# Three edits to a hybrid diffusion step in split fp32: another pool for modulated tiles, an operand built beside the output projection, gate and residual one chunk sooner

## The chip, the cores and the metric

The kernel runs on one core of one Trainium2 chip. The metric is the device time of one launch in microseconds (us), the median of several runs; lower is better. The engines of the core work side by side: PE (TensorE) does the matmuls, PEld is its weight load, DVE is VectorE, ACT is ScalarE, POOL is GpSimd, SP is SyncE. Each engine runs its own instructions in order and waits on semaphores for the others. In this kernel SP issues the loads from HBM and POOL issues most of the stores and a few loads.

## The reference

One layer of a network with three kinds of token mixing, for 128 context tokens and 2048 latent tokens of width D = 1024, all in fp32. What matters here is its second half:

```
mix = concat(A, B, C) @ w_out                       # 1024 x 1024
x   = x + gate1 * mix                               # called x1 in the kernel
h   = rmsnorm(x) * (1 + scale2) + shift2            # the modulated tile
x   = x + gate2 * (square(relu(h @ w_ff1)) @ w_ff2) # 1024 x 4096, 4096 x 1024
y   = rmsnorm(x, final_g)
```

shift2, scale2, gate1 and gate2 are vectors of 1024, one set for the context tokens and one for the latent ones. A, B and C are gated linear attention, a depthwise convolution and a gated MLP over chunks; they come ahead of the stages that the change touches.

## The kernel before

**Tiles and arithmetic.** The 2176 tokens are 17 tiles of 128: t = 0 is the context, t = 1 to 16 are latent. Every fp32 matmul operand is held as a pair: hi, a copy on ACT that is rounded to the matmul's type, and lo, the source minus hi, subtracted on DVE or POOL. One product is three matmuls (`mm3`: hi x hi, hi x lo, lo x hi), so lo of the left operand is first wanted by the third matmul. Function `split` (L169 on) does the copy (L171) and the subtract (L172); `split_in_place` (L1168 on) does it with lo over the source (L1169, L1170).

**Stages.** In the profiled execution the projection of the inputs and the mixing take the time up to about 731 us, the output projection lasts to about 1031, FF1 (h @ w_ff1, with a Strassen-like form of seven products p = 0 to 6 on sums of operand blocks) to about 1743, FF2 to 2492, and a tail follows.

**Output projection** (`out_proj`, L754 on, called for t = 16 down to 0). For each tile it loads the mixed tile `mt` (L766), copies it to `mh` on ACT (L767), subtracts `ml` on POOL (L768), loads `x1` (L770), and takes a buffer `tmp` (L772). Then 16 units of 3 matmuls run, 8 for each half of the columns. After each half `done` multiplies by the gate row into `tmp` (L777) and adds into `x1` (L778), on DVE; after the second half it stores x1 (L780), squares and sums (L64), takes the reciprocal root (L160, L161) and scales x1 into `tmp` (L784). The modulated tile is made in `tmp` beside the NEXT tile's matmuls: at unit 12 and after unit 16 `h2_half` transposes four 128 x 128 blocks on PE (L129) and applies scale and shift with four ACT instructions (L64). Tiles go in pairs, even t then odd t. After the odd tile's second half `h2_pair` (L815 on) forms four combinations of both tiles on DVE (L827 to L830) into two tiles `cb`, and POOL issues stores of all to `tb_d` (L822, L831 to L834); these are FF1's right operands, for i = 0 to 6.

**What sets the order.** The program is written as loops, and a list scheduler orders each engine's instructions when the program is built. The buffers of one tag in a pool are handed out strictly in the order in which the program first writes them: an instruction that first writes a buffer is placed after the one that first writes the buffer handed out before it. The load of `mt` is the first write of its buffer. The hand-out orders the placing alone: a load on SP may run as soon as its own buffer is free. `weave` (L149) runs the units in turn and the side items at their unit numbers.

**Pools.** Tag w (23 buffers of 128 x 1024, `wtile`) holds w_out (16), the gate rows, `x1` and `tmp`. Tag T (18, `tunit`) holds `mt`, `mh`, `ml` and `cb`, later FF1's right operands of i < 4, and in FF2 the accumulators `ya`. When the output projection is done pool wp is closed (L1152) and pool fp lies over its memory: tag u (12, `uunit`) for right operands of i >= 4 and for FF2's left operands F, tag v (11, `wunit`) for weights. The first buffers of fp are handed out only behind the last release of wp. `raw` (3 buffers) stages loads, `cacc` (2) and `xp` (3) are work tiles.

**FF1's start** (L1286 on). Left operands are loaded and split (`left_operand`, L1180), the 14 halves of right operands (7 i, two kk each) are loaded by POOL (L1176) and split in place.

**FF2** (`ff2_units`, L1385, loop L1419). 8 chunks c of 512 rows of w_ff2; in each, 5 blocks b of token tiles: four of 4 tiles and one of 1 tile (t = 0). A tile is 24 matmuls in 8 units, 12 for each half of the columns. The four weight pairs of the next chunk are loaded and split during blocks 0 to 3 (`load_ff2`, L1337, split L171 and L172). The left operands F of a block are two pairs, loaded (`load_f`, L1354) and split in place; three such sets fit in tag u. Each half is evicted by ACT in chunk 0 (L1403) and added into `ya` by DVE after that (L1405). In the last chunk `finish` (L1360) multiplies the half by gate2 (L1372), adds x1 (L1373), squares (L1376), and after the second half takes the root and scales twice (L67), then stores. It loads x1 again from `x1_d` into a `raw` buffer.

The functions that the diff touches:

Of the kernel before, what the change touches and what calls it, by code (L numbers as in the profile page):

```python
# [8 lines left out]
F32 = mybir.dt.float32  # L9
# [9 lines left out]
D = 1024  # L19
# [24 lines left out]
def tile_hybrid(  # L44
# [60 lines left out]
    def xp_tile():  # L105
        return rawp.tile([P, 1536], F32, tag="xp", name="xp", bufs=3)
# [4 lines left out]
    def wtile(dt=F32R):  # L111
        return wp.tile([P, D], dt, tag="w", name="w", bufs=23)
# [36 lines left out]
    def weave(units, items):  # L149

        items = sorted(items, key=lambda it: it[0])
        for i, u in enumerate(units):
            while items and items[0][0] <= i:
                items.pop(0)[1]()
            u()
        for _, f in items:
            f()
# [596 lines left out]
    def out_proj(t):  # L754

        cd = 0 if t == 0 else 1
        if cd not in g1rows:
            g1rows[cd] = wtile(F32)
            gate_row(g1rows[cd], 0, cd)
        cq.finish(t)  # L760
        if t == NT - 1:
            hu, mt = hunit()
            mh, ml = hu[:, 0], hu[:, 1]
        else:
            mt, mh, ml = tunit(F32), tunit(), tunit()
        ld.dma_start(out=mt, in_=mix_d[t].rearrange("p k t -> p (k t)"))  # L766
        S.copy(out=mh, in_=mt)  # L767
        G.tensor_tensor(out=ml, in0=mt, in1=mh.bitcast(F32), op=ALU.subtract)  # L768
        x1 = wtile(F32)
        ld.dma_start(out=x1, in_=x_rows(t))  # L770

        tmp = xp_tile()[:, 0:D] if t == 0 else wtile(F32)  # L772

        def done(half):
            def f(pz):
                fs = slice(half * 512, (half + 1) * 512)
                V.tensor_tensor(out=tmp[:, fs], in0=pz, in1=g1rows[cd][:, fs], op=ALU.mult)  # L777
                V.tensor_tensor(out=x1[:, fs], in0=tmp[:, fs], in1=x1[:, fs], op=ALU.add)  # L778
                if half == 1:
                    st.dma_start(out=x1_d[t], in_=x1)  # L780
                    ssq = const.tile([P, 1], F32, name="ssq3", bufs=2)
                    act(tmp, x1, AF.Square, accum_out=ssq)
                    rstd_of(ssq, ssq, D)
                    S.mul(tmp, x1, ssq)  # L784
            return f

        def lhs(k):
            ks = slice(k * P, (k + 1) * P)
            return mh[:, ks], ml[:, ks]

        units = []
        for half in range(2):
            units += mm_units(512, lhs, of_pairs(wo[half]), done(half))

        hs = []

        def h2_half(kq):
            pt = gbank()
            for kk in range(4):
                k = kq * 4 + kk  # L800
                tr(pt[:, kk * P:(kk + 1) * P], tmp[:, k * P:(k + 1) * P])
            hf = tmp.rearrange("p (k t) -> p k t", k=KD)
            for kk in range(4):
                k = kq * 4 + kk
                act(hf[:, k, :], pt[:, kk * P:(kk + 1) * P], AF.Identity, scale=s2[:, k, cd:cd + 1],
                    bias=modc[:, KD + k, cd:cd + 1])
            ks = slice(kq * 4, kq * 4 + 4)
            if t == 0:
                split(hc[0][:, ks], hc[1][:, ks], hf[:, ks])
            elif kq == 1:  # L810
                h2_pair(t, hf)

        return units, [(12, lambda: h2_half(0)), (16, lambda: h2_half(1))]
# [22 lines left out]
    def ticks(n, rate):  # L836
        return [(p_ + 0.5, lambda: cq.tick(rate / n)) for p_ in range(n)]
# [3 lines left out]
    with ExitStack() as p2:  # L841
# [110 lines left out]
        class ConvQueue:  # L952
# [27 lines left out]
            def finish(self, t):  # L980

                while any(t in g[0] for g in self.groups):
                    self.tick(1.0)
                self.credit = 0.0
                while any(t in d[1] for d in self.due):
                    self.tick(0.0)
# [155 lines left out]
    hbs.close()  # L1142
    tp.append(tps.enter_context(tc.tile_pool(name="tp", bufs=1, side="right", reuse_waits="tile")))
    hc = []

    for t in range(NT - 2, -1, -1):
        units, nxt_late = out_proj(t)
        if t == 0:
            hc += [tunit().rearrange("p (k t) -> p k t", k=KD) for _ in range(2)]
        weave(units, late3 + ticks(16, RATE3))  # L1150
        late3 = nxt_late
    wps.close()  # L1152

# [6 lines left out]
    def wunit(dt=F32R):  # L1160
        return fp.tile([P, D], dt, tag="v", name="v", bufs=11)
# [2 lines left out]

    def split_in_place(hi, lo):  # L1168
        S.copy(out=hi, in_=lo.bitcast(F32))  # L1169
        V.tensor_tensor(out=lo, in0=lo.bitcast(F32), in1=hi.bitcast(F32), op=ALU.subtract)  # L1170

    def right_operand(g, i, kk, dst):

        unit = tunit if i < 4 else uunit
        hi, lo = unit(), unit()
        st.dma_start(out=lo.bitcast(F32).rearrange("p (k n) -> p k n", k=2), in_=tb_d[g][:, i, 2 * kk:2 * kk + 2])  # L1176
        split_in_place(hi, lo)
        dst[i, kk] = (hi, lo)

    def left_operand(i):  # L1180

# [101 lines left out]

        return [lambda k=k: unit(k) for k in range(KD)], turn

    TB = [{}, {}]  # L1286
    ORDER = [(i, kk) for i in range(7) for kk in range(2)]
    w, steps = left_operand(0)
    steps[0]()
    steps[1]()  # L1290
    for i, kk in ORDER[:2]:
        right_operand(0, i, kk, TB[0])
    steps[2]()
    for i, kk in ORDER[2:4]:
        right_operand(0, i, kk, TB[0])
# [41 lines left out]
    def load_ff2(f):  # L1337
        rw = raw()
        ld.dma_start(out=rw, in_=w_ff2[0, f * P:(f + 1) * P, :])
        hi, lo = wunit(), wunit()  # L1340
        split(hi, lo, rw)
        return hi, lo

    def load_f(c, b):
# [12 lines left out]

        return out, [lambda p=p: step(p) for p in range(CF // 2)]

    def finish(t, y):  # L1360

        ssq = const.tile([P, 2], F32, name="ssq4", bufs=4)
        x1 = raw()
        ld.dma_start(out=x1, in_=x1_d[t])
        g2c = g2r
        if t == 0:
            g2c = raw()
            gate_row(g2c, 1, 0)

        def half(h):  # L1370
            fs = slice(h * 512, (h + 1) * 512)
            V.tensor_tensor(out=y[:, fs], in0=y[:, fs], in1=g2c[:, fs], op=ALU.mult)  # L1372
            V.tensor_tensor(out=y[:, fs], in0=x1[:, fs], in1=y[:, fs], op=ALU.add)  # L1373
            act(x1[:, fs], y[:, fs], AF.Square, accum_out=ssq[:, h:h + 1])
            if h == 1:
                V.tensor_tensor(out=ssq[:, 0:1], in0=ssq[:, 0:1], in1=ssq[:, 1:2], op=ALU.add)  # L1376
                rstd_of(ssq[:, 0:1], ssq[:, 0:1], D)
                for i in range(2):
                    fs = slice(i * 512, (i + 1) * 512)
                    stt(y[:, fs], y[:, fs], ssq[:, 0:1], fgr[:, fs], ALU.mult, ALU.mult)  # L1380
                    ld.dma_start(out=y_rows(t)[:, fs], in_=y[:, fs])

        return half

    def ff2_units(c, b, F, w2):  # L1385
        units = []
        for j, t in enumerate(blocks[b]):
            js = slice(j * P, (j + 1) * P)
            fin = []

            def unit(h, f, t=t, js=js, fin=fin, box=[]):
                hs = slice(h * 512, (h + 1) * 512)
                if f == 0:
                    box.append((zbank if h == 0 else gbank)())
                py = box[-1]
                fh, fl = F[f // 2]
                mm3(py, fh[:, f % 2, js], fl[:, f % 2, js], w2[f][0][:, hs], w2[f][1][:, hs], f == 0, f == CF - 1)
                if f < CF - 1:
                    return
                if c == 0:  # L1400
                    if h == 0:
                        ya[t] = tunit(F32)
                    S.copy(out=ya[t][:, hs], in_=py)  # L1403
                else:
                    V.tensor_tensor(out=ya[t][:, hs], in0=py, in1=ya[t][:, hs], op=ALU.add)  # L1405
                if c == NC_ - 1:
                    if h == 0:
                        fin.append(finish(t, ya[t]))
                    fin[0](h)

            units += [lambda h=h, f=f, unit=unit: unit(h, f) for h in range(2) for f in range(CF)]
        return units
# [5 lines left out]
    steps[1]()  # L1418
    for c in range(NC_):  # L1419
        w2n = []  # L1420
        for b in range(5):
            units = ff2_units(c, b, F, w2)
            items = []
            nb, ncx = (b + 1, c) if b < 4 else (0, c + 1)
            if ncx < NC_:
                F, steps = load_f(ncx, nb)
                items += zip((3.5, 9.5) if b < 4 else (0, 1), steps)
            if c + 1 < NC_ and b < 4:
                items.append((14.5, lambda f=(c + 1) * CF + b: w2n.append(load_ff2(f))))
            weave(units, items)  # L1430
        w2 = w2n
# [30 lines left out]
```

## Time and profile before

| | us |
|---|---|
| median of 3 runs | 2510.64 |
| lowest and highest run | 2509.28, 2511.52 |
| the profiled execution, its own time | 2516.82 |
| its span, first to last instruction | 2515.1 |

| engine | busy us | share of the span |
|---|---|---|
| PE | 2349.2 | 93% |
| DVE | 1472.8 | 59% |
| ACT | 890.1 | 35% |
| POOL | 436.8 | 17% |

Mean granted PE clock 0.966. The times of rows are microseconds from the start of the span. In a timeline a row is start, length, engine, line, operation, output and inputs by the program's names, shapes, how many instructions run together; in brackets how long the engine sat idle before it and what ended that. Rows of one engine stand for its order; rows of different engines overlap.

### The profile page before, as it was taken

The page shows a single profiled execution, that of the slowest core. Times are in us where ns is not written, and L with a number is a line of the kernel's source. Part 1 is how long each engine was busy: PE and PEld are TensorE (multiplying, and loading weights), DVE is VectorE, ACT ScalarE, POOL GpSimd, SP SyncE. Part 2 cuts the span into 40 slices and gives each one's busy share as a digit, 9 for nine tenths or more (in the row PEclk, how much of TensorE's full clock was granted, in tenths as well). Part 3 has the DMA queues.
Part 4 walks back from the last instruction along what each step waited for, and adds up shares of the span by engine and source line. Part 5 has one row for each costly group of instructions (what it writes and reads, how often), then busy time and mean ns, then how long its engine had stood idle before and what let it go on. Part 6 is the DMA issues. An engine that isn't in the chain of part 4 may idle for free.

```text
span 2515.1 us, 32249 instructions
## 1 busy us (share of the span) xinstructions
PE 2349.2 (93%) x12402; PEld 1921.3 (76%) x12402; DVE 1472.8 (59%) x2492; ACT 890.1 (35%) x1710; POOL 436.8 (17%) x593
## 2 busy tenths in 40 slices
PE   6999999999988777699999899999999999999996
PEld 5788887777766555488888788887878888888885
DVE  5987755878885663555555766655134344344387
ACT  4666764333444344432333433333321011011032
POOL 2332325444423333200000100000000000000001
PEclk9999999999998888799999999999999999999998
DMA  8655635333443444522233533335122122122154
GB/s 277 236 194 195 219 107 165 121 125 130 144 153 130 151 148 167 202 97 91 103 103 105 198 101 106 123 106 176 38 84 88 38 88 84 38 88 84 38 196 152
DMA packets 145321, 326.24 MB, mean 130 GB/s; under 512 B 13349, under 2 KB 58703, under 8 KB 141584
## 3 DMA queue, kind: packets, MB, share of 16 engines
q1 hardware_dynamic: 110640, 191.73, 23.5%
q0 software_dynamic: 34528, 132.46, 14.6%
q8 instruction: 97, 1.59, 0.3%
q14 instruction: 56, 0.46, 0.1%
HBM read 213.24 MB, written 110.90 MB: 129 GB/s over the span
## 4 chain that ended last, share of the span: by engine, by line
PE 62%; DVE 12%; issue 5%; POOL 4%; DMA 2%; ACT 2%; POOLq 0%; SPq 0%; DVEq 0%; ACTq 0%
PE z L126 42%; PE g L126 19%; DVE cacc L67 5%; DMA u<-tb_d 1%; PE g L129 1%; DVE T L67 1%; POOL T L768 1%; DMA u<-f_d 1%; POOL ssq L161 1%; DVE uv L67 1%; DVE T L1373 1%; POOL mv L161 1%; POOL s L161 1%; DVE T L1405 1%; DVE T L1372 0%
## 5 line engine op out<-in xcount | busy, mean ns | idle before, releaser
L126 PE MATMUL z<-w,hb 128*128 128x512 f32 (+1 forms) x2438 | 551.1, 372 | 5.7 <-ACT w L171 3.2
L126 PEld LDWEIGHTS z<-w,hb 128*128 128x128 f32 x2438 | 412.6, 192 | 81.8 <-issue 5.0
L126 PE MATMUL z<-v,u 128*128 128x512 f32 x1632 | 395.0, 391 | 3.5 <-DVE v L172 1.5
L126 PE MATMUL g<-v,u 128*128 128x512 f32 x1632 | 393.6, 391 | 0.0
L126 PEld LDWEIGHTS z<-v,u 128*128 128x128 f32 x1632 | 306.7, 188 | 69.4 <-DVE v L172 2.3
L126 PEld LDWEIGHTS g<-v,u 128*128 128x128 f32 x1632 | 307.7, 189 | 64.0
L126 PE MATMUL z<-T,v 128*128 128x512 f32 x1152 | 286.6, 401 | 29.2 <-ACT T L1169 22.7
L126 PEld LDWEIGHTS z<-T,v 128*128 128x128 f32 x1152 | 217.3, 190 | 84.4 <-ACT T L1169 25.3
L126 PE MATMUL z<-w,T 128*128 128x512 f32 x768 | 212.1, 431 | 65.9 <-ACT T L767 51.2
L126 PE MATMUL z<-u,v 128*128 128x512 f32 x1152 | 269.2, 392 | 0.0
L1169 ACT CAST u<-u 128x1024 fp32r<-128x1024 f32 (+1 forms) x92 | 86.3, 939 | 489.2 <-DMA u<-f_d 330.1
L126 PEld LDWEIGHTS z<-u,v 128*128 128x128 f32 x1152 | 217.6, 189 | 46.5
L126 PEld LDWEIGHTS z<-w,T 128*128 128x128 f32 x768 | 153.4, 207 | 106.1 <-ACT T L767 53.3
L67 DVE SCALAR_TENSOR_TENSOR cacc<-xp,wd,cacc 128x512 f32<-128x512 f32 (+2 forms) x360 | 233.8, 703 | 0.0
L1405 DVE TENSOR_TENSOR T<-z,T 128x512 f32<-128x512 f32 x119 | 82.2, 690 | 160.8 <-PE z L126 160.7
L161 POOL TENSOR_TENSOR ssq<-ssq,mhalf 128x1 f32<-128x1 f32 x51 | 39.0, 765 | 767.8 <-DVE ssq L160 752.4
L1405 DVE TENSOR_TENSOR T<-g,T 128x512 f32<-128x512 f32 x119 | 82.1, 690 | 151.3 <-PE g L126 151.3
L1170 DVE TENSOR_TENSOR u<-u 128x1024 fp32r<-128x1024 f32 (+1 forms) x92 | 99.6, 1082 | 104.8 <-ACT u L1169 104.7
L172 DVE TENSOR_TENSOR v<-raw,v 128x1024 fp32r<-128x1024 f32 x96 | 116.4, 1222 | 64.9 <-PE z L126 60.9
L171 ACT CAST v<-raw 128x1024 fp32r<-128x1024 f32 x96 | 100.3, 1051 | 94.3 <-issue 59.4
L172 DVE TENSOR_TENSOR v<-cacc,v 128x1024 fp32r<-128x1024 f32 x64 | 78.3, 1225 | 87.3 <-PE z L126 87.3
L1245 POOL DMA_DIRECT2D f_d<-xp x32 | 17.1, 533 | 519.9 <-DVE xp L67 519.9
(266 smaller groups left out, 2754.8 us busy)
## 6 DMA issues: line engine op xcount, KB each, us to landing
raw<-in_w_ff_dram SPq DMA_DIRECT2D x96, 512.0 KB
f_d<-xp POOLq DMA_DIRECT2D x64, 512.0 KB, 3.4
u<-f_d SPq DMA_DIRECT2D x64, 512.0 KB
raw<-in_w_mod_dram SPq DMA_DIRECT2D x32, 512.0 KB
hb<-hT_d POOLq DMA_DIRECT2D x15, 1024.0 KB, 5.6
hT_d<-hb POOLq DMA_DIRECT2D x13, 1024.0 KB, 6.7
ss_d<-ss POOLq DMA_DIRECT2D x34, 256.0 KB, 4.0
r<-ss_d SPq DMA_DIRECT2D x34, 256.0 KB
```

The costliest lines, as they stand in the source:

```text
L67: return V.scalar_tensor_tensor(out=out, in0=in0, scalar=scalar, in1=in1, op0=op0, op1=op1)
L126: tc.keep_in_program_order(T.matmul(out, lhsT, rhs, start=start, stop=stop, skip_group_check=read))
L129: tc.keep_in_program_order(T.transpose(out, in_, ident if idn is None else idn))
L161: G.tensor_tensor(out=out, in0=out, in1=mhalf[:, 0:out.shape[-1]], op=ALU.pow)
L171: order(S.copy(out=hi, in_=src))
L172: order(V.tensor_tensor(out=lo, in0=src, in1=hi.bitcast(F32), op=ALU.subtract))
L768: G.tensor_tensor(out=ml, in0=mt, in1=mh.bitcast(F32), op=ALU.subtract)
L1169: S.copy(out=hi, in_=lo.bitcast(F32))
L1170: V.tensor_tensor(out=lo, in0=lo.bitcast(F32), in1=hi.bitcast(F32), op=ALU.subtract)
L1245: st.dma_start(out=f_d[i][g][:, 0], in_=f0)
L1373: V.tensor_tensor(out=y[:, fs], in0=x1[:, fs], in1=y[:, fs], op=ALU.add)
L1405: V.tensor_tensor(out=ya[t][:, hs], in0=py, in1=ya[t][:, hs], op=ALU.add)
```

## The change

It has three parts in the code, and the third has two effects.

1. `tmp` of tiles 15 to 1 is a T buffer instead of a w buffer; tile 16 keeps w and tile 0 keeps xp.
2. `split_in_place` and `right_operand` are defined ahead of the output projection's loop. The right operand of i = 0 (both kk: two loads by POOL, two copies, two subtracts, four T buffers) is made at units 10 and 14 of tile 2; FF1's start no longer makes it.
3. In FF2 every fourth weight pair (f % 4 == 3) takes u buffers instead of v buffers. The gate and the residual of chunks 0 to 6 are applied at the end of chunk 6 (`residual`: the sum is multiplied by gate2, x1 is added), and in chunk 7 each half is multiplied by gate2 straight from its PSUM bank into a `raw` buffer and added to `ya`. Gate2 of the context is held in a T buffer from chunk 6 on.

```diff
-        tmp = xp_tile()[:, 0:D] if t == 0 else wtile(F32)
+        tmp = xp_tile()[:, 0:D] if t == 0 else wtile(F32) if t == NT - 1 else tunit(F32)
...
     for t in range(NT - 2, -1, -1):
         units, nxt_late = out_proj(t)
         if t == 0:
             hc += [tunit().rearrange("p (k t) -> p k t", k=KD) for _ in range(2)]
-        weave(units, late3 + ticks(16, RATE3))
+        items = late3 + ticks(16, RATE3)
+        if t == 2:
+            items += [(10 + 4 * kk, lambda kk=kk: right_operand(0, 0, kk, TB[0])) for kk in range(2)]
+        weave(units, items)
         late3 = nxt_late
     wps.close()
...
     steps[0]()
     steps[1]()
-    for i, kk in ORDER[:2]:
-        right_operand(0, i, kk, TB[0])
     steps[2]()
...
-        hi, lo = wunit(), wunit()
+        unit = uunit if f % CF == CF - 1 else wunit
+        hi, lo = unit(), unit()
         split(hi, lo, rw)
...
+    g2rows = {1: g2r}
+
+    def residual(t, y):
+        x1 = raw()
+        ld.dma_start(out=x1, in_=x1_d[t])
+
+        def half(h):
+            fs = slice(h * 512, (h + 1) * 512)
+            V.tensor_tensor(out=y[:, fs], in0=y[:, fs], in1=g2rows[min(t, 1)][:, fs], op=ALU.mult)
+            V.tensor_tensor(out=y[:, fs], in0=x1[:, fs], in1=y[:, fs], op=ALU.add)
+        return half
+
     def finish(t, y):
         ssq = const.tile([P, 2], F32, name="ssq4", bufs=4)
-        x1 = raw()
-        ld.dma_start(out=x1, in_=x1_d[t])
-        g2c = g2r
-        if t == 0:
-            g2c = raw()
-            gate_row(g2c, 1, 0)
-        def half(h):
+        tmp = raw()
+        def half(h, py):
             fs = slice(h * 512, (h + 1) * 512)
-            V.tensor_tensor(out=y[:, fs], in0=y[:, fs], in1=g2c[:, fs], op=ALU.mult)
-            V.tensor_tensor(out=y[:, fs], in0=x1[:, fs], in1=y[:, fs], op=ALU.add)
-            act(x1[:, fs], y[:, fs], AF.Square, accum_out=ssq[:, h:h + 1])
+            V.tensor_tensor(out=tmp[:, fs], in0=py, in1=g2rows[min(t, 1)][:, fs], op=ALU.mult)
+            V.tensor_tensor(out=y[:, fs], in0=y[:, fs], in1=tmp[:, fs], op=ALU.add)
+            act(tmp[:, fs], y[:, fs], AF.Square, accum_out=ssq[:, h:h + 1])
...
+                if c == NC_ - 1:
+                    if h == 0:
+                        fin.append(finish(t, ya[t]))
+                    fin[0](h, py)
+                    return
                 if c == 0:
...
                 else:
                     V.tensor_tensor(out=ya[t][:, hs], in0=py, in1=ya[t][:, hs], op=ALU.add)
-                if c == NC_ - 1:
+                if c == NC_ - 2:
                     if h == 0:
-                        fin.append(finish(t, ya[t]))
+                        fin.append(residual(t, ya[t]))
                     fin[0](h)
...
     for c in range(NC_):
         w2n = []
+        if c == NC_ - 2:
+            g2rows[0] = tunit(F32)
+            gate_row(g2rows[0], 1, 0)
```

## Rows read from the trace of the kernel before

**Rows 1.** The page: busy time of the engines, and the granted PE clock in slices

```profile
PE 2349.2 (93%) x12402; PEld 1921.3 (76%) x12402; DVE 1472.8 (59%) x2492; ACT 890.1 (35%) x1710; POOL 436.8 (17%) x593
...
PEclk9999999999998888799999999999999999999998
```

**Rows 2.** Waits of PE, 700 to 1110 us: total us, times, longest us

```profile
PE z L126 <- ACT T L767: 51.2, 8, 8.6
PE z L126 <- ACT T L1169: 18.2, 3, 15.1
PE z L126 <- POOL T L768: 14.7, 8, 2.2
```

**Rows 3.** Timeline of the output projection, one pause and the odd tile behind it

```profile
857.58 1.98 ACT L767 CAST T<-T 128x1024 fp32r<-128x1024 f32 x2
857.79 7.08 DVE L67 SCALAR_TENSOR_TENSOR cacc<-xp,wd,cacc 128x512 f32<-128x512 f32 x3
858.66 1.22 PE L126 MATMUL z<-w,T 128*128 128x512 f32 x2 [5.74 <-ACT T L767]
859.65 4.66 POOL L768 TENSOR_TENSOR T<-T 128x1024 fp32r<-128x1024 f32 x2
862.06 10.08 PE L126 MATMUL z<-w,T 128*128 128x512 f32 x34 [2.18 <-POOL T L768]
...
869.38 0.69 DVE L777 TENSOR_TENSOR w<-z,w 128x512 f32<-128x512 f32 x1 [4.51 <-PE z L126]
872.67 1.50 ACT L64 ACTIVATE w<-g,modc,s 128x128 f32<-128x128 f32 x4 [13.12 <-PE g L129]
875.56 8.61 PE L126 MATMUL z<-w,T 128*128 128x512 f32 x36
876.12 0.69 DVE L778 TENSOR_TENSOR w<-w 128x512 f32<-128x512 f32 x1
```

**Rows 4.** DMA issues of the page: KB each, median us to landing

```profile
f_d<-xp POOLq DMA_DIRECT2D x64, 512.0 KB, 3.4
```

**Rows 5.** Windows behind that pause: length, PE, PEld, DVE, ACT, POOL busy, PEclk, DMA

```profile
862.00:866.00 4.00, 3.94 (x9) 3.18 (x10) 2.87 (x1) 0.00 (x0) 2.31 (x2) 0.50 1.02 351
866.00:870.00 4.00, 4.00 (x18) 3.25 (x17) 0.62 (x1) 0.00 (x0) 0.00 (x0) 0.96 0.46 189
```

**Rows 6.** Timeline from the output projection into FF1

```profile
1036.33 2.36 DVE L172 TENSOR_TENSOR v<-raw,v 128x1024 fp32r<-128x1024 f32 x2 [0.78 <-ACT v L171]
1061.34 1.05 ACT L1169 CAST T<-T 128x1024 fp32r<-128x1024 f32 x1
1065.33 1.22 DVE L1170 TENSOR_TENSOR T<-T 128x1024 fp32r<-128x1024 f32 x1
1069.95 1.06 ACT L1169 CAST T<-T 128x1024 fp32r<-128x1024 f32 x1
1071.09 1.23 DVE L1170 TENSOR_TENSOR T<-T 128x1024 fp32r<-128x1024 f32 x1 [2.28 <-issue]
```

**Rows 7.** Timeline of FF2, the start of a block

```profile
1907.92 1.89 SPq L1354 DMA_DIRECT2D u<-f_d  x2
1909.31 2.88 PE L126 MATMUL z<-v,u 128*128 128x512 f32 x12
1911.69 1.05 ACT L1169 CAST u<-u 128x1024 fp32r<-128x1024 f32 x1 [21.62 <-DMA u<-f_d]
1913.76 1.05 ACT L1169 CAST u<-u 128x1024 fp32r<-128x1024 f32 x1 [1.02 <-DMA u<-f_d]
```

**Rows 8.** Windows of one chunk of FF2 and of the last; columns as in rows 5

```profile
2303.00:2396.00 93.00, 93.00 (x412) 77.05 (x411) 37.83 (x48) 13.24 (x14) 0.00 (x0) 1.00 0.22 71
2397.00:2492.00 95.00, 94.55 (x418) 78.02 (x416) 87.65 (x159) 28.53 (x68) 11.28 (x14) 1.00 0.57 193
```

**Rows 9.** Timeline of the tail

```profile
2488.67 2.88 PE L126 MATMUL g<-v,u 128*128 128x512 f32 x12
2503.03 0.69 DVE L1373 TENSOR_TENSOR T<-raw,T 128x512 f32<-128x512 f32 x1
```

More of the change, by code (lines that the diff above doesn't have):

```diff
@@ L1144, in tile_hybrid @@
     hc = []
-    for t in range(NT - 2, -1, -1):
-        units, nxt_late = out_proj(t)
-        if t == 0:
-            hc += [tunit().rearrange("p (k t) -> p k t", k=KD) for _ in range(2)]
-        weave(units, late3 + ticks(16, RATE3))
-        late3 = nxt_late
-    wps.close()
-    fp = ctx.enter_context(tc.tile_pool(name="fp", bufs=1, reuse_waits="tile"))
-    def uunit(dt=F32R):
-        return fp.tile([P, D], dt, tag="u", name="u", bufs=12)
-    def wunit(dt=F32R):
-        return fp.tile([P, D], dt, tag="v", name="v", bufs=11)
-    NP = DFF // 256
+    TB = [{}, {}]
     def split_in_place(hi, lo):
@@ L1178, in right_operand, with uunit, wunit @@
         dst[i, kk] = (hi, lo)
+    for t in range(NT - 2, -1, -1):
+        units, nxt_late = out_proj(t)
+        if t == 0:
+            hc += [tunit().rearrange("p (k t) -> p k t", k=KD) for _ in range(2)]
+        items = late3 + ticks(16, RATE3)
+        if t == 2:
+            items += [(10 + 4 * kk, lambda kk=kk: right_operand(0, 0, kk, TB[0])) for kk in range(2)]
+        weave(units, items)
+        late3 = nxt_late
+    wps.close()
+    fp = ctx.enter_context(tc.tile_pool(name="fp", bufs=1, reuse_waits="tile"))
+    def uunit(dt=F32R):
+        return fp.tile([P, D], dt, tag="u", name="u", bufs=12)
+    def wunit(dt=F32R):
+        return fp.tile([P, D], dt, tag="v", name="v", bufs=11)
+    NP = DFF // 256
     def left_operand(i):
@@ L1284, in ff1_context @@
         return [lambda k=k: unit(k) for k in range(KD)], turn
-    TB = [{}, {}]
     ORDER = [(i, kk) for i in range(7) for kk in range(2)]
@@ L1358, in load_f @@
         return out, [lambda p=p: step(p) for p in range(CF // 2)]
+    g2rows = {1: g2r}
[7 more added lines that the diff above has]
+        return half
     def finish(t, y):
         ssq = const.tile([P, 2], F32, name="ssq4", bufs=4)
-        x1 = raw()
-        ld.dma_start(out=x1, in_=x1_d[t])
-        g2c = g2r
-        if t == 0:
-            g2c = raw()
-            gate_row(g2c, 1, 0)
-        def half(h):
+        tmp = raw()
+        def half(h, py):
             fs = slice(h * 512, (h + 1) * 512)
-            V.tensor_tensor(out=y[:, fs], in0=y[:, fs], in1=g2c[:, fs], op=ALU.mult)
-            V.tensor_tensor(out=y[:, fs], in0=x1[:, fs], in1=y[:, fs], op=ALU.add)
-            act(x1[:, fs], y[:, fs], AF.Square, accum_out=ssq[:, h:h + 1])
+            V.tensor_tensor(out=tmp[:, fs], in0=py, in1=g2rows[min(t, 1)][:, fs], op=ALU.mult)
+            V.tensor_tensor(out=y[:, fs], in0=y[:, fs], in1=tmp[:, fs], op=ALU.add)
+            act(tmp[:, fs], y[:, fs], AF.Square, accum_out=ssq[:, h:h + 1])
             if h == 1:
```

## The prediction

> **What bounds the kernel now.** I read the page first: PE is busy for 2349.2 of 2515.1 us, and in 40 slices the granted clock is 0.9 or more but for five, the 13th to the 17th (755 to 1069 us, mostly the output projection), and the last [rows 1]. So most of the kernel can only get faster where PE does less, and the change takes no matmul away. What it can touch is where PE stands still. The profiled execution took 2516.82 us, 6.18 over the median of 2510.64, and its span is 2515.1; I make the sum on the span and carry the difference over to the median. About 0.2%, 5 us, is what a measurement of this kernel can tell from no change.
>
> The waits of PE from the output projection to FF1 come next [rows 2]. PE waits 8 times for the copy of a mixed tile (51.2 us, 6.4 each), 8 times for its subtract (14.7 us, 1.8 each), and once for 15.1 us where FF1 begins. The timeline shows why there are 8 and not 16 [rows 3]: the two copies of a pair of tiles run back to back at 857.58, behind the odd tile's combinations, and PE pauses once a pair, for 5.74 and 2.18 us. The even tile's operands are ready with the odd tile's, so its first matmul at 875.56 follows without a wait.
>
> In FF2 the window of a chunk is 93.00 us of PE in 93.00, with DVE at 37.83; in the last chunk DVE is busy for 87.65 of 95 [rows 8]. PE's last matmuls end at 2488.67 + 2.88 = 2491.55, but the last addition of x1 starts at 2503.03 [rows 9]: DVE is 11.5 us behind, and the tail from there to 2515.1 is a chain of square, root, scaling and store.
>
> **Part 1, the T buffers.** No instruction is added. What moves is the order of placing. T buffers are handed out in the order of their first writes. Now tmp of an odd tile stands in that row ahead of the even tile's mt, and tmp's first write is the gate multiply L777 in the middle of the odd tile, at 869.38 [rows 3]. So the even tile's load and copy can't be placed in the pause any more; they come behind 869.38. On SP the load is no cost, since it runs ahead as soon as its buffer is free. On ACT the copy lands near the four modulations of 872.67 to 874.17 [rows 3], 3.29 us after the multiply. A 512 KB transfer lands in 3.4 us [rows 4], so the builder may put the copy on either side of them.
> Behind them: copy 874.2 to 875.2 (1.0 each by the pair of 1.98), subtract on POOL 2.33 (4.66 for two) to 877.6. The even tile starts at 875.56 and wants lo with its third matmul, two matmuls of 0.23 later, at 876.0. PE pauses 1.6 us, 8 times (tiles 14, 12, to 0): +13. Ahead of them: nothing, 0. I take +13, since 3.4 is over 3.29, and keep 0 as the low end. The odd tile's own pause stays: its copy still stands behind the combinations, and PE restarts with the first copy and the first subtract, which remain, so a gain is left out.
> Each new pause may also cost the clock. After the pause at 862.06 the granted clock is 0.50 of 2.4 GHz (1.2 GHz) from 862 to 866, with 9 matmuls in 3.94 us, where the next 4 us hold 18 at 0.96 [rows 5]. At 0.23 us each those 9 would have taken 2.0, so 1.9 is lost. A pause of 1.6 us is far shorter than 5.74 + 2.18, so I take 0 of it and keep 1.9 x 8 = 15 for the high end.
> The even tile's subtract now runs beside L778, the add of x1, at 876.12 [rows 3]. Beside two subtracts on POOL three taps on DVE took 7.08 us [rows 3], where a half-width operation takes 0.69. So L778 may be held up to 2.3 us. Its result is wanted by the transposes twelve units on, at 875.56 + 36 x 0.23, some 8 us later, behind square, root and scaling: taken as 0.
> The Trainium skill ("SBUF — State Buffer", section "Who interferes with whom") says that a DVE operation on two SBUF operands and one of GpSimd shut each other out. The three taps agree; by that rule alone the sum would gain at most that 2.3 us a pair if the chain behind L778 had no slack.
>
> **Part 2, the first right operand.** Two loads on POOL, two copies (1.05), two subtracts (1.22) on ACT and DVE [rows 6] go into tile 2. POOL's stores of the pair lie behind them in its queue; ACT stood idle for 13.12 us ahead of the modulations [rows 3], so the copies are hidden there: 0, with +2 at most if a load holds POOL ahead of a pair's stores. At FF1's start 14 halves are loaded and split, and the steady run waits for the late ones that sit in T: the last split starts at 1071.09. With two halves gone, T's last split stands where the one at 1065.33 stood: -5.8. The least is two subtracts, -2.4; the most is the distance of the copies, 1069.95 - 1061.34, -8.6 [rows 6]. The wait of 15.1 itself [rows 2] is filled from 1037.5, where the first weights are split [rows 6], by the first product's 12 matmuls, but that end is set by the later halves, so nothing more is counted.
>
> **Part 3, the weight pair in u.** Tag u has 12 buffers; a set F takes 4, so three sets fit. Four now go to the fourth weight pairs of two chunks, and two sets stay. Then F for the next chunk's block 0 can only be loaded when block 3 is done, at the start of block 4, which is one tile, 24 matmuls of 0.227, 5.44 us. The rows of a block's start show what such a load takes: issued 1907.92, first matmul of the block 1909.31, copies at 1911.69 and 1913.76, 2.4 and 4.45 after it [rows 7]. With copy 1.05 and subtract 1.22 the first half is ready at 2.4 + 1.05 + 1.22 = 4.7, under 5.44. The second has hi at 5.5 (wanted at 5.44 + 6 x 0.227 = 6.8) and lo at 6.8 (wanted at 7.25). It just fits, but evictions of 0.69 and a weight subtract of 1.22 stand on DVE in the same 5 us: 0 to 1.8 us (the 1.22 and one 0.69 that can stand ahead) at each of 7 boundaries, 0 to +12.6. I take 0.5 each, +3.5, nearer to the rows' bare fit. In exchange v is less short (12 wanted of 11, instead of 16), which cost nothing before: PE has no wait there [rows 8].
>
> **Part 4, gate and residual.** In chunk 6 DVE gets 17 x 4 operations of 0.69 at most, 47 us on 37.83 of 93 [rows 8]: 85, still under PE, 0. On SP 17 loads of x1 come ahead of F and weight loads, and one that waits for a raw buffer holds those behind it for a tile at most, 5.44 us, while F is loaded up to a block ahead: 0, up to +2 at the last boundary. In chunk 7 DVE loses 2 of its half-width operations a tile, 34 x 0.69 = 23 of 87.65 [rows 8], and fits under PE. The last half is then multiplied when PE ends, at 2491.6, and added from 2492.3, where the addition starts at 2503.03 now [rows 9]; what follows is the same. -10.7, with -8 if four half-width operations of earlier tiles, 0.69 each, stand ahead, and -11.5 as the most, the whole lag.
>
> **Sum.** +13 - 5.8 + 3.5 - 10.7 = 0.0. On the median: 2511.
>
> **The rivals.** A, **no new pauses**: the builder puts the copies ahead of the modulations, or the modulations wait for them. For it: 3.29 against 3.4 is close, and ACT is idle there for 13.12 us [rows 3]. Against it: the builder put both copies behind L784 in the pair's pause. Then 2511 - 13 = 2498, faster.
> B, **the chunk boundary**, the other side: F's second half waits behind DVE at each of 7 boundaries, 1.8 instead of 0.5 each: 2511 + 9 = 2520, slower. It decides as soon as DVE's extra work in block 4 is over 0.4 us ahead of F's subtracts (7.25 - 6.8). Against it: DVE is at 41% there [rows 8].
> C, **the clock**: each of the 8 new pauses lowers it as at 862 [rows 5], 8 x 1.9 = 15 more: 2526. Against it: 1.6 us is a fifth of the pause that did so.
> The Trainium skill ("TensorE: Matmul & The Clock Gate", Part 1) says that the array falls back to half its clock after idleness and takes it up again after sustained work. Rows 5 agree for the long pause; no row has one of 1.6 us alone.
> D, **the last chunk does not speed up**: DVE still trails because scaling of earlier tiles is placed ahead. That would leave 5 of the 10.7: 2516. It speaks against D that DVE falls to 65 of 95.
>
> **How the numbers follow.** Forecast 0.43, own range 2504 to 2518; A 0.32; B 0.14; C 0.06; D 0.05. Faster by over 0.2% (under 2505.6): A, 0.31, and 0.08 of the forecast, 0.39. Slower (over 2515.7): B 0.13, C 0.06, D 0.03 and 0.10 of the forecast, 0.32. The rest, 0.29, is within it. For 8 in 10 the range takes in A with its -8.6 not quite reached, down to 2495, and B, up to 2523; C and the far ends are left out.
>
> **What would show it.** Right: PE waits for L767 and L768 at even tiles too, with up to 16 waits and short ones of 1 to 2 us in mid pair; two copies a pair no longer together; FF1's first matmuls near 1037 on the old scale, and the last T split some 6 us sooner behind the output projection; DVE under 70 us in the last chunk and its last addition within 1 us of PE's end. Wrong: no waits at even tiles (A), PE waits for L1169 or L1170 every 92.5 us in FF2 (B), a granted clock under 0.9 within the pairs (C), a lag at the end (D), or DVE over 95% in chunk 6.

## The result, and the profile after

The changed kernel takes 2528.39 us (4 runs, 2527.14 to 2529.54); the kernel before, in the same comparison, 2511.08 (2509.28 to 2516.19). The ratio is 1.0066 [1.0048, 1.0083]: **slower by 0.7%**, where no change was forecast, and above the range. In the 18 runs of the kernel before that stand beside the first four experiments its median is 2513.23, so the loss is 15 to 17 us.

The page after:

```profile
PE 2358.3 (93%) x12402; PEld 1922.5 (76%) x12402; DVE 1499.7 (59%) x2526; ACT 891.3 (35%) x1710; POOL 433.6 (17%) x593
...
PEclk9999999999988888799999999999999999999998
```

Beside [rows 1] PE is busy for 9 us more with the same 12402 matmuls, and the granted clock is under 0.9 in the 12th to the 17th slice instead of the 13th to the 17th. That does not say which stage is longer, or why. A view of one line with its first and last start per group cuts the kernel into stages:

```profile
L126 PE MATMUL z<-v,u x1224: 387/389/796, 1754.0 to 2504.2; 128*128 128x512 f32 x175
...
L126 PE MATMUL z<-w,T x768: 387/395/796, 750.8 to 1044.1; 128*128 128x512 f32 x192
...
L126 PE MATMUL g<-u x408: 387/389/398, 1767.4 to 2507.6; 128*128 128x512 f32 x136
```

The output projection (z<-w,T) runs from 750.8 to 1044.1, FF2 from 1754.0 to 2507.6. The same view of every kernel gives the table below: start of the first matmul to start of the last for the output projection and for FF2, what lies between for FF1, and what lies behind to the span's end. All are profiled executions. The kernel before is there twice: its first profile, on which the prediction was made, is of an execution 6 us over the median, and its second has a span of 2508.9.

| kernel | up to | output proj. | FF1 | FF2 | end | span |
|---|---|---|---|---|---|---|
| before, profile of the prediction | 751.6 | 278.6 | 714.5 | 746.5 | 23.9 | 2515.1 |
| before again (e11) | 748.4 | 279.0 | 713.9 | 744.1 | 23.5 | 2508.9 |
| **changed** | 750.8 | 293.3 | 709.9 | 753.6 | 19.9 | 2527.5 |
| e1 tmp in w | 748.7 | 279.0 | 709.7 | 751.9 | 19.9 | 2509.2 |
| e2 operands ahead | 749.4 | 284.6 | 710.3 | 751.9 | 20.0 | 2516.2 |
| e3 weights all in v | 749.0 | 293.2 | 711.0 | 743.9 | 19.6 | 2516.7 |
| e4 scaling later | 748.1 | 293.6 | 709.6 | 753.8 | 14.8 | 2519.9 |
| e5 cb in w | 752.0 | 241.9 | 702.7 | 753.9 | 15.2 | 2465.7 |
| e6 mended | 751.5 | 280.6 | 709.5 | 744.0 | 15.8 | 2501.4 |
| e7 mended, cb in w | 748.9 | 239.8 | 705.7 | 744.0 | 11.0 | 2449.4 |
| e8 operand back | 750.0 | 291.7 | 712.3 | 753.2 | 20.0 | 2527.2 |
| e9 in halves | 751.2 | 278.1 | 710.7 | 754.3 | 19.9 | 2514.2 |
| e10 all mended | 750.2 | 223.9 | 703.9 | 744.0 | 10.0 | 2432.0 |

Against e11 the change costs 14.3 in the output projection, gives 4.0 in FF1, costs 9.5 in FF2 and gives 3.6 at the end; with 2.4 in the stages ahead, which it doesn't touch, that is the 18.6 between the spans.

**Output projection.** The waits of PE from 690 to 1110 us, as in [rows 2]:

```profile
PE z L126 <- ACT T L767: 53.6, 8, 8.8
PE z L126 <- POOL T L768: 24.1, 15, 2.3
PE g L126 <- ACT T L1148: 6.7, 2, 3.8
PE z L126 <- ACT v L171: 5.5, 1, 5.5
```

The copy is waited for 8 times as before, for 2.4 us more; the subtract 15 times instead of 8, for 9.4 us more. The seven new waits stand at seven of the eight even tiles and last 1.1 to 1.6 us (at 914 us, the eighth, there is none). The timeline at an even tile, where [rows 3] have no wait at 875.56:

```profile
877.90 1.51 ACT L64 ACTIVATE T<-g,modc,s 128x128 f32<-128x128 f32 x4 [14.77 <-PE g L129]
879.28 1.06 ACT L767 CAST T<-T 128x1024 fp32r<-128x1024 f32 x1
880.42 2.37 POOL L768 TENSOR_TENSOR T<-T 128x1024 fp32r<-128x1024 f32 x1 [13.89 <-ACT T L767]
...
880.80 0.70 PE L126 MATMUL z<-w,T 128*128 128x512 f32 x2
...
881.37 1.97 DVE L778 TENSOR_TENSOR w<-T,w 128x512 f32<-128x512 f32 x1
882.84 8.16 PE L126 MATMUL z<-w,T 128*128 128x512 f32 x34 [1.34 <-POOL T L768]
```

The copy is alone now and stands behind the four modulations; the subtract is 1.3 us late for the third matmul. L778, beside the subtract, takes 1.97 us instead of 0.69 and is not waited for. The window right behind the pause, with columns as in [rows 5]:

```profile
882.84:886.84 4.00, 4.00 (x17) 3.30 (x18) 2.71 (x6) 2.44 (x4) 2.46 (x3) 1.00 0.34 130
```

The granted clock is 1.00, and so it is in the 4 us behind each of the other six short pauses: they do not lower it, as the long pause of [rows 5] did.

**FF2's start.** Before, both loads of the first F were issued together; after, the second goes out behind a weight load, and its copy is PE's wait of 4.61:

```profile
1737.15 1.47 SPq L1354 DMA_DIRECT2D u<-f_d  x2
```

```profile
1747.48 0.57 SPq L1357 DMA_DIRECT2D u<-f_d  x1
...
1752.44 0.33 SPq L1341 DMA_DIRECT2D raw<-in_w_ff_dram  x1
1752.88 0.55 SPq L1357 DMA_DIRECT2D u<-f_d  x1
...
1760.01 1.04 ACT L1148 CAST u<-u 128x1024 fp32r<-128x1024 f32 x1 [3.06 <-DMA u<-f_d]
...
1761.11 2.05 PE L126 MATMUL z<-v,u 128*128 128x512 f32 x3 [4.61 <-ACT u L1148]
```

**A chunk's end in FF2.** The weight load of PE (PEld) waits twice for the subtract of F, 0.30 and 0.51, partly behind matmuls that still run; the first nine matmuls of the chunk take 2.73 instead of 2.20:

```profile
2134.95 2.73 PE L126 MATMUL z<-v,u 128*128 128x512 f32 x9
...
2135.44 1.23 PEld L126 LDWEIGHTS z<-v,u 128*128 128x128 f32 x6 [0.30 <-DVE u L1149]
...
2137.17 0.19 PEld L126 LDWEIGHTS z<-v,u 128*128 128x128 f32 x1 [0.51 <-DVE u L1149]
```

The starts of the first matmuls of two chunks lie 93.03 apart from the third chunk on, where they lay 92.48 apart before.

**The last tile of the last chunk.** PE ends at 2507.10 + 0.84 = 2507.94:

```profile
2507.10 0.84 PE L126 MATMUL g<-u 128*128 128x512 f32 x3
...
2512.06 1.41 DVE L67 SCALAR_TENSOR_TENSOR T<-T,ssq,cacc 128x512 f32<-128x512 f32 x2 [0.75 <-POOL ssq L161]
2513.39 0.68 DVE L1384 TENSOR_TENSOR raw<-z,T 128x512 f32<-128x512 f32 x1
...
2515.44 0.69 DVE L1385 TENSOR_TENSOR T<-T,raw 128x512 f32<-128x512 f32 x1
...
2518.02 1.41 DVE L67 SCALAR_TENSOR_TENSOR T<-T,ssq,cacc 128x512 f32<-128x512 f32 x2 [0.75 <-POOL ssq L161]
```

The first multiply of the last tile (2513.39) stands right behind the scaling of the tile before (2512.06), which has waited 0.75 us for the root on POOL and, before that, for the squares on ACT. From one scaling to the next are 2518.02 - 2512.06 = 5.96 us, over PE's 5.44. The last addition starts 7.5 us behind PE's end ([rows 9]: 11.5). The whole chunk, columns as in [rows 5]:

```profile
2414.00:2507.00 93.00, 92.33 (x406) 75.82 (x406) 74.85 (x135) 29.35 (x69) 8.76 (x15) 1.00 0.34 116
```

DVE is busy for 74.85 us here, 4.4 for each of 17 tiles, and PE takes 5.44.

### The profile page after: what moved, and what is told of

It is laid out like the page before. It is cut to its first block, busy times and chain, and to the rows that moved or that the text cites. A ratio compares the mean times of both kernels' runs of the same rounds, so it can differ in the third digit from the quotient of the medians.

```text
span 2527.5 us, 32291 instructions
## 1 busy us (share of the span) xinstructions
PE 2358.3 (93%) x12402; PEld 1922.5 (76%) x12402; DVE 1499.7 (59%) x2526; ACT 891.3 (35%) x1710; POOL 433.6 (17%) x593
## 5 line engine op out<-in xcount | busy, mean ns | idle before, releaser
L126 PE MATMUL z<-v,u 128*128 128x512 f32 x1224 | 304.4, 391 | 7.2 <-ACT u L1148 4.6
L126 PE MATMUL g<-v,u 128*128 128x512 f32 x1224 | 300.7, 390 | 0.0
L126 PEld LDWEIGHTS z<-v,u 128*128 128x128 f32 x1224 | 229.3, 188 | 60.9 <-DVE u L1149 8.6
L126 PEld LDWEIGHTS g<-v,u 128*128 128x128 f32 x1224 | 230.8, 189 | 48.2
L67 DVE SCALAR_TENSOR_TENSOR cacc<-xp,wd,cacc 128x512 f32<-128x512 f32 (+2 forms) x360 | 226.6, 682 | 0.0
L1422 DVE TENSOR_TENSOR T<-z,T 128x512 f32<-128x512 f32 x102 | 70.4, 690 | 137.5 <-PE z L126 137.1
L172 DVE TENSOR_TENSOR v<-raw,v 128x1024 fp32r<-128x1024 f32 x88 | 107.3, 1221 | 64.0 <-PE z L126 60.2
L1422 DVE TENSOR_TENSOR T<-g,T 128x512 f32<-128x512 f32 x102 | 70.3, 689 | 125.9 <-PE g L126 125.9
L171 ACT CAST v<-raw 128x1024 fp32r<-128x1024 f32 x88 | 92.4, 1051 | 92.0 <-issue 55.5
L126 PE MATMUL z<-u 128*128 128x512 f32 x408 | 115.3, 391 | 0.0
```

What stands on the lines that cost most here:

```text
L67: return V.scalar_tensor_tensor(out=out, in0=in0, scalar=scalar, in1=in1, op0=op0, op1=op1)
L126: tc.keep_in_program_order(T.matmul(out, lhsT, rhs, start=start, stop=stop, skip_group_check=read))
L171: order(S.copy(out=hi, in_=src))
L172: order(V.tensor_tensor(out=lo, in0=src, in1=hi.bitcast(F32), op=ALU.subtract))
```

## The experiments

**e1, tmp back in w.** One line of the change undone.

```diff
-        tmp = xp_tile()[:, 0:D] if t == 0 else wtile(F32) if t == NT - 1 else tunit(F32)
+        tmp = xp_tile()[:, 0:D] if t == 0 else wtile(F32)
```

> The changed kernel (2528.4 us) with tmp of tiles 15 to 1 back in tag w, all else kept. Theory (the order of the first writes sets the copies): the two copies of a pair are placed together again, the 8 waits of 1.3 to 1.4 us at even tiles are gone, the output projection is 13.9 us shorter, about 2514.5 us. Rival (the stage is longer because conversions and DVE work beside POOL got slower, whatever the order): the waits at even tiles go, but less than half of the 13.9 comes back, over 2521 us.

Measured 2512.60 us, 1.0002 [0.9993, 1.0012] of the kernel before, and an output projection of 279.0. PE's waits there:

```profile
PE z L126 <- ACT T L767: 51.2, 8, 8.6
PE z L126 <- POOL T L768: 14.7, 8, 2.2
```

They are those of [rows 2] to the tenth. Part 1 is the whole loss of that stage.

**e2, operands ahead, tmp still in T.** The load, copy and subtract became a function `operands(t)`, called at unit 5 of the odd tile for the even one.

```diff
...
+        if t % 2 == 1:
+            items.append((5, lambda t=t - 1: ready.update({t: operands(t)})))
```

> The changed kernel with tmp still in tag T, but with the even tile's load, copy and subtract written in the program at unit 5 of the odd tile, ahead of the first write of the odd tile's tmp. Theory (order of first writes): as fast as with tmp in w, 8 pauses a pair fewer, about 2514.5 us. Rival (it is the place of tmp, the fuller T ring or a shared port, that costs): no change, 2528 us.

Measured 2518.40 us, 1.0025 [1.0014, 1.0036].

```profile
PE z L126 <- ACT T L764: 51.9, 8, 8.4
PE z L126 <- POOL T L765: 15.9, 8, 2.6
PE g L129 <- ACT raw L64: 2.2, 1, 2.2
```

Again 8 and 8 waits, with tmp in T: the waits at even tiles come from the order of the first writes, not from the place. The stage is 5.6 longer than in e1 all the same. The edit also asks for the even tile's convolution (`cq.finish`) half a tile sooner, and a wait of PE in the convolution's transposes appears (2.2); over the stage PE stands still 2.6 longer and is busy 3.0 longer than in e1, and why it is busy longer was not traced.

**e3, FF2's weights all in v.**

```diff
-        unit = uunit if f % CF == CF - 1 else wunit
-        hi, lo = unit(), unit()
+        hi, lo = wunit(), wunit()
```

> The changed kernel with all weight pairs of FF2 in tag v again. Theory (tag u loses its third set of F, at FF2's start and at each chunk's end): FF2 from its first matmul to its last is 746.9 us as before instead of 753.9, no gap of 0.55 us at the boundaries and none of 4.6 us at the start: about 2521.4 us. Rival (only the boundaries are from tag u, the 4.6 us at the start come from FF1's later end): 3.2 back, about 2525 us.

Measured 2519.47 us, 1.0034 [1.0021, 1.0047]; FF2 743.9 instead of 753.6, chunks 92.48 apart. Its start:

```profile
1753.15 0.73 PE L126 MATMUL z<-v,u 128*128 128x512 f32 x2 [0.92 <-ACT u L1148]
1754.41 1.85 PE L126 MATMUL z<-v,u 128*128 128x512 f32 x6 [0.53 <-DVE u L1149]
1757.29 1.20 PE L126 MATMUL z<-v,u 128*128 128x512 f32 x4 [1.02 <-DVE u L1149]
```

The wait of 4.61 is gone as well as the loss at the chunks' ends: both were from tag u. The rival falls.

**e4, scaling one half later.** The root and the scaling of a tile, as a function `scale`, are called behind the next tile's first half, and the DVE operations concerned are held in that order.

```diff
...
+            if h == (1 if t == 0 else 0) and owed:
+                owed.pop(0)()
             if h == 1:
...
+                owed.append(scale)
+                if t == 0:
+                    owed.pop(0)()
...
```

> The changed kernel, but in the last chunk the root and the scaling of a tile stand on DVE behind the first half's multiply and add of the next tile, in an order that is fixed (for the last tile, behind its second half). The same operations. Theory (DVE falls behind since each tile's first multiply is queued behind a scaling that waits for square and root, 5.96 us a tile against PE's 5.44): DVE keeps pace, the last addition of x1 follows PE's end by about 1 us, the stretch from PE's end to the span's end falls from 19.6 to about 13, 2522 us. Rival (DVE's own work a tile is too long): the lag at the end stays over 5 us, 2527 us or more.

Measured 2523.38 us, 1.0049 [1.0034, 1.0064]; the end falls from 19.9 to 14.8.

```profile
2504.62 0.84 PE L126 MATMUL g<-u 128*128 128x512 f32 x3
...
2506.23 0.69 DVE L1386 TENSOR_TENSOR T<-T,raw 128x512 f32<-128x512 f32 x1
...
2507.93 1.42 DVE L67 SCALAR_TENSOR_TENSOR T<-T,ssq,cacc 128x512 f32<-128x512 f32 x2 [0.75 <-POOL ssq L1398]
```

The last addition follows PE's end (2505.46) by 0.77 us. The same operations keep pace in another order: DVE's order was the cause, not its load. Of the 6.7 so won, 1.5 go to the scaling of the tile before, which now stands at 2507.93 in the last tile's own chain.

**e5, cb in w.** One line; the long pause of a pair was there before the change too.

```diff
-        cb = [tunit(F32).rearrange("p (i k t) -> p i k t", i=2, k=4) for _ in range(2)]
+        cb = [wtile(F32).rearrange("p (i k t) -> p i k t", i=2, k=4) for _ in range(2)]
```

> The changed kernel with the two tiles cb of a pair in tag w instead of T (where tmp has made room); nothing else. Theory (the long pause of a pair is the same thing: the odd tile's mt stands behind cb in the order of T's first writes): the 8 pauses of 5.3 + 2.2 us are gone, every tile has a short one of some 1.4 us, since its mt now stands behind the first write of the tile before's tmp. The output projection takes about 16 x (11.8 + 1.4) = 211 us instead of 293.7, and the kernel about 2446 us. Rival (the odd tile's copy waits for something else: the root of the tile before, the convolution that fills its mixed tile, or the stores): the long pauses stay, over 2515 us.

Measured 2466.97 us, 0.9809 [0.9794, 0.9823], 21 more than expected. The output projection is 241.9.

```profile
PE z L126 <- POOL T L768: 23.8, 16, 2.4
PE z L126 <- ACT T L767: 13.4, 3, 6.0
```

Of the 8 waits for the copy 3 are left, and the subtract is waited for at each of 16 tiles, 1.5 on the mean: most of the long pauses were the order of first writes, as the theory has it. A late load was not what held the copies: in the kernel before, the loads for the two copies at 857.58 [rows 3] are issued 33 us earlier:

```profile
824.07 2.69 SPq L766 DMA_DIRECT2D T<-mix_d  x2
```

Tiles without a long wait take 13.6 us, near the 13.2 expected; what is over lies in some of 14 to 21. What those wait for beyond the row was not tried.

**e6, mended:** tmp in w, weights in v, scaling later (for the last tile too behind its first half).

> The changed kernel with tmp back in w, FF2's weights all in v, and the scaling of the last chunk one half later in a fixed order (for the last tile as for the others): what is left of the change is the first right operand and the gate and residual one chunk sooner. Theory (the costs lie in separate stages and add up): 2528.4 - 15.8 - 8.9 - 6.3 = 2497 us, 14 to 16 us under the kernel before. Rival (they overlap: what one part gives back another takes): over 2503 us.

Measured 2503.26 us, 0.9953 [0.9937, 0.9970]. That is just over the rival's mark, and 6 over the theory. The stages say where: the output projection is 1.6 over e1, which stays open, and the end 1.0 over e4, since the last tile's second half now queues behind the scaling of the tile before (the last addition is 3.3 behind PE's end, 0.8 in e4): that last touch at e4 was a loss. And FF2 was already 1.7 shorter in e1 than in the changed kernel, a gain that e3 brings too and that the sum counted twice. So the parts are nearly separate by the stages, but the total alone does not show it.

**e7, mended, with cb in w.**

> The kernel with cb in tag w and tmp in T, FF2's weights all in v, the scaling one half later. Theory: the gain of cb in w and the two others add up, 2446 - 8.9 - 6.3 = 2431 us. Rival (a shorter output projection only moves the wait to the start of FF1, whose operands and stores come through the same queues): over 2445 us.

Measured 2453.79 us, 0.9757 [0.9743, 0.9772]. It is 13.2 under e5, where 15.2 was expected; the rest of the 23 over the theory is e5's own miss. FF1 did not take the gain back: 705.7 against 709.9.

**e8, the first right operand back at FF1's start.**

> The changed kernel with the first right operand made at FF1's start again, all else kept. Theory (its early making is what shortens the stretch between the last matmul of the output projection and the first of FF2 from 714.1 to 709.6): that stretch is 714 again and the kernel 2533 us. Rival (the stretch is shorter for another reason, such as less left in w when its pool closes): it stays at 710, 2528 us.

Measured 2529.96 us, 1.0061 [1.0046, 1.0076], not told apart from the changed kernel by the intervals. The stretch is 712.3, between the two: 2.4 of the 4.0 are from the operand, and where the other 1.6 comes from stays open. T's last split, in e8 and in the changed kernel, and a window behind the latter:

```profile
1083.37 1.23 DVE L1149 TENSOR_TENSOR T<-T 128x1024 fp32r<-128x1024 f32 x1 [2.22 <-ACT T L1148]
```

```profile
1081.59 1.23 DVE L1149 TENSOR_TENSOR T<-T 128x1024 fp32r<-128x1024 f32 x1 [0.42 <-ACT T L1148]
```

```profile
1084.00:1088.00 4.00, 4.00 (x12) 3.14 (x11) 1.69 (x2) 1.53 (x2) 0.00 (x0) 0.58 0.25 73
```

From the start of the output projection's last matmul (1041.7 and 1044.1) it is 41.7 us in e8, 37.5 in the changed kernel and 40.9 in both profiles of the kernel before. So the early operand brings the split 4.2 sooner, but the granted clock behind it is 0.58, where e8 has 1.00, and the next 12 matmuls take 4.39 instead of 2.91. The output projection is 1.6 shorter without the operand (it is 293.2 to 293.6 in the changed kernel, e3 and e4), so little is left of part 2.

**e9, conversions in halves.**

```diff
-        S.copy(out=mh, in_=mt)
-        G.tensor_tensor(out=ml, in0=mt, in1=mh.bitcast(F32), op=ALU.subtract)
+        for c0 in (0, 512):
+            cs = slice(c0, c0 + 512)
+            S.copy(out=mh[:, cs], in_=mt[:, cs])
+            G.tensor_tensor(out=ml[:, cs], in0=mt[:, cs], in1=mh[:, cs].bitcast(F32), op=ALU.subtract)
```

> The changed kernel with the copy and the subtract of a mixed tile each in two halves of the columns (first half copied, first half subtracted, then the second). Theory (PE pauses at an even tile for as long as a whole copy and a whole subtract behind the four modulations take, though its first matmuls want 128 of the 1024 columns): the first half of lo is there about 1.7 us sooner, the waits of 1.3 to 1.4 us at even tiles go, and of the odd tiles' waits for the subtract (2.2 each) about 1.2 and for the copy 0.5; 8 x 1.4 + 8 x 1.7 = 25 us less at most, 2505 to 2512. Rival (the pause is POOL's, whose stores and shared port hold the subtract): less than 5 us, over 2523 us.

Measured 2511.43 us, 0.9995 [0.9985, 1.0005].

```profile
PE z L126 <- ACT T L769: 50.2, 9, 9.5
PE z L126 <- POOL T L770: 11.2, 8, 1.9
```

The waits for the subtract are half of the 24.1. Of the even tiles two still wait for it, one for 1.5 us (behind a new wait of 1.9 for its copy) and one for 0.2. The stage is 278.1, so this alone pays for part 1.

**e10, all mended:** e7 with halves, and the last tile as in e4.

> The kernel of the run with cb in w, weights in v and scaling one half later, with copies and subtracts in halves, and with the last tile's two halves ahead of the scaling of the tile before. Theory: its 16 short waits of 1.4 us go too and the end is 1 us sooner, 2453.8 - 22 - 1 = 2431 us. Rival (with the pauses gone DVE, which makes the convolution beside it, is what the stage waits for): over 2445 us.

Measured 2433.39 us (2432.64 to 2434.59), 0.9686 [0.9672, 0.9700]: 3.1% under the kernel before, the best here.

```profile
PE z L126 <- ACT T L769: 15.5, 3, 8.1
...
PE z L126 <- POOL T L770: 7.7, 7, 2.2
```

The 16 waits for the subtract have become 7; three long ones for the copy are left, as in e5.

**e11, the kernel before again.**

> The kernel before, unchanged, for a second profile. Its first has some 5.6 us at the very end in which nothing runs and no transfer moves, as nearly all profiles here; two have under 1 us. Theory (it comes and goes by execution): the span without it is 2507 +- 3 us, and it may be there or not. Rival (it belongs to the kernel): it is there again, some 5 us.

Its span is 2508.94, and the quiet end is there again: from the last DVE operation to the end of the span 8.09 us, as in its first profile. The theory that it comes and goes falls.

## Why the prediction was wrong

- **Part 1, +13:** the mechanism named is right: the copy behind the modulations, and a wait at even tiles. e1 and e2 show it. That the size, 14.3 against e11, is so near is partly luck: the waits are 1.1 to 1.6 us at seven tiles, not 1.6 at eight, 9.4 in all; 2.4 of longer waits for the copy and 2.4 of longer busy PE in the stage, neither of them in the sum, make up the rest. The condition of rival C is not met behind the short pauses, where the clock is 1.00. Luck was also the choice of the far side of the modulations by 3.4 over 3.29: 3.4 is what a store of `f_d` takes [rows 4], and in the trace after the load for the copy at 879.28 was issued at 862.61, so no landing decided it there; what the builder reckoned with no run shows.
- **Part 2, -5.8:** too large. The stretch lost 4.0, of which e8 gives 2.4 to the operand, the low end of the bounds; the output projection paid part of it back. The step that put T's last split where an earlier one stood counted a position as time: the split comes 3.4 sooner than before (4.2 than in e8), not 5.8, and clock takes 1.5 of that back (e8). The one wait of 15 us at FF1's start is gone, but the first product's later operands are still waited for (6.7 for two T copies in the rows after).
- **Part 3, +3.5:** at the chunks' ends it is right: 0.55 at each of five, 1.26 at the last (the second chunk is 0.7 shorter than in e3), by the subtracts of F as worked out. But the step saw only the ring in its steady state. At FF2's start the same fourth pair stands ahead of F's second half in tag u; the first chunk takes 101.13 us to the next one's start, 94.93 in e3. That is 6.2; the wait of 4.61 is in it, and clock, granted at 0.53 from 1761 to 1767 us and at 1.00 in e3 (e1 and e2, with the same weights in u, have 99.41 and 99.21). The prediction had nothing for that place. With it part 3 costs 9.5.
- **Part 4, -10.7:** the step that failed worst, 3.6 to 4.0 instead. DVE was to be busy for 65 us of the last chunk and is for 74.85; but at 4.4 a tile it stays under PE's 5.44, and that much is right: e4 runs the same operations in time. But the next tile's multiply was taken to start when PE ends, although the scaling ahead of it in DVE's queue waits for ACT and POOL. Sum of busy time is not the period of a chain. Rival D named this mechanism and put 5 us and one chance in twenty on it; the runs give 6.7.
- **The whole:** against the profile of the prediction the misses are 14.7 - 13, 5.8 - 4.6, 7.1 - 3.5 and 10.7 - 4.0, all to one side, 13 us. The rest of the 17 is that profile: it lay 6 us over the median, 3.2 of that ahead of the output projection and 2.4 in FF2, so one profile was not enough to say what is normal.

## What to carry to other kernels

When a pool hands out buffers in the order of first writes, moving a late-written tile into a ring places every conversion behind it in that ring later, even where the load runs early; ask for each ring whose first write comes late, in the steady state and at each stage's start. An engine with time to spare still sets the pace if one of its in-order instructions waits for a chain through other engines; count the chain from one such instruction to the next, and put it behind the next tile's work. A consumer that starts on an eighth of a tile should not wait for the conversion of all of it.

## What was not expected of the hardware

The same instructions at FF2's start ran at different clocks in two executions of the kernel before, with much the same waits. Windows of its first profile, then of its second, whose first FF2 matmuls start at 1744.68 and 1741.35 (columns as in rows 5):

```profile
1744.00:1750.00 6.00, 4.26 (x11) 2.47 (x12) 4.10 (x4) 3.01 (x4) 0.77 (x2) 0.74 0.97 343
1750.00:1756.00 6.00, 6.00 (x20) 4.73 (x19) 1.22 (x1) 2.45 (x4) 0.00 (x0) 0.69 0.98 310
```

```profile
1742.00:1748.00 6.00, 4.46 (x18) 3.08 (x18) 3.42 (x4) 2.97 (x4) 0.53 (x1) 1.00 0.96 334
1748.00:1754.00 6.00, 6.00 (x29) 4.95 (x27) 2.62 (x3) 3.31 (x5) 0.00 (x0) 1.00 0.85 274
```

The granted clock is 0.74 and 0.69 in one and 1.00 in the other, where 29 matmuls fit in place of 20; the two FF2 differ by 2.4 us.

From the last DVE operation to the span's end it is 8.1 us in every profile with cb in T and 3.3 in the three with cb in w (e5, e7, e10), though the last transfers are alike. These 4.8 us are part of the gain of those three. The instructions of the program's last line, of the changed kernel and then of e5, which differs in one line, show what lies there (x3: shortest, median and longest in ns, first and last start):

```profile
L1478 POOLq DRAIN  x3: 46/98/9325, 2517.4 to 2527.2; - x3
```

```profile
L1478 POOLq DRAIN  x3: 46/97/1568, 2460.4 to 2465.4; - x3
```

A drain on POOL, issued beside its last root, lasts 9.3 us in one and 1.6 in the other. It is 9.3 in all ten profiles with cb in T, where it ends 0.8 us before the span does, and 1.6 to 1.8 in the three with cb in w. So the long end is a wait on POOL; why cb's place sets its length stays open.
